# Two-block layer on one core: attention values taken transposed in column halves, softmax weights put on the exponentials

## Chip, cores and metric

The kernel runs on one core of one Trainium2 chip, as one launch. The metric is the device time in microseconds (us); where several runs are shown it is their median. A profile shows one execution of the program, with its own time and span.

## What is computed

The layer has two blocks. Only the second one's attention is touched. Its input is 512 tokens in four tiles of 128. In short, from the reference:

```python
# NSA: 8 heads of 64 in 2 groups; three softmaxes per head, each with a gate
o = g[..., 0:1] * o_cmp + g[..., 1:2] * o_slc + g[..., 2:3] * o_win
# o_cmp: 31 compressed keys; o_slc, o_win: causal over up to 512 keys
# MLA: 8 heads, query/key width 96, value width 64
p = masked_softmax(s, key_idx[None, :] <= tc[:, None])
o_mla = jnp.einsum('bhqk,bkhd->bqhd', p, v)
mixed = jnp.concatenate([o_nsa * silu(z_nsa), o_mla * silu(z_mla)], axis=-1)
x = x + gate[:, None, :] * (mixed @ w_out[l])
```

For 512 keys the selection takes all blocks, so the branches slc and win are both plain causal attention with their own keys and values.

## The kernel before

The second block is `block2`. Its projections come first; then `attention()` (L1524) runs woven with `fill()` (L1809), and last `out_tiles((2, 3))` makes the output of two token tiles. TensorE's order inside the woven part is the program's order (`tc.manual_schedule` with that engine, L1842); the other engines are ordered by the scheduler.

**Attention.** The work is a list of units, `ORDER_2` (L1150). A `Unit` (L1364) is two heads of one token tile `tt` in one branch; it sees n = (tt+1)*128 keys. There are 8 units per tile for the two NSA branches ("key") and 4 per tile for MLA ("mla"), so 48 units, and one `Blocks` unit (L1401) per tile for the 31 compressed keys of all 8 heads. A unit has three steps:

- `scores`: two matmuls and two mask matmuls into two "sc" banks, two maxima on VectorE (L1380), two exponentials on ScalarE with their sums (L1383);
- `turn`: 128x128 transposes of the exponentials on TensorE (L1391), evacuated by `K.copy`, which takes ScalarE (L63) and VectorE (L65) by turns;
- `values`: per head and 128 keys one matmul (L1398) with the transposed exponentials as the stationary operand and 64 columns of values as the moving one. The result has tokens on partitions.

When the units of a branch are through, `nsa_done` (L1455) takes reciprocals of the sums, multiplies them by the gates and weighs the 128x512 result on VectorE (L1359); GpSimd adds the branches (L1467). For MLA `finish` (L1498) does the like (L1499, L1501). `mix` (L1548) then transposes four 128x128 pieces on TensorE (L1552), multiplies them by z on VectorE (L1555) and splits the product in two parts for the output projection.

**Pipeline.** `attention()` issues in one step: `turn` of the unit before, `scores` of this unit, fill, `values` of the unit two before (LAG = 1).

**Fill.** `fill()` is the other TensorE work: `latents` (7 projections, the first two of which give the gates), `blocks` (compressed keys; with a Silu at L1673 and a rope before the transpose L1700), four columns of z and a Silu of all of it (L1807), `heads` (MLA queries, keys, values), four more columns of z and the second Silu, then `mix` of the NSA tiles and `out_tiles((0, 1))`, which needs both NSA and MLA of tiles 0 and 1. A column is 24 matmuls of 512 columns (L105 to L107), written as 8 pieces of 0.64 us.

`weave_us` (L178) sets how they alternate: each step of attention yields a number of us (`u.us`, twice the number of `FB` in `ORDER_2`) and the fill is advanced until its own written costs have eaten it. Where a step needs something of the fill (`needs`: "gates", "blocks", "heads", "z") it yields 1.0 until that is done. Where the fill needs attention's results it yields `None`, and the step then gets no fill:

```python
while tt == 1 and ("mla", 1) not in done:
    yield None
if tt == 1:
    yield from out_tiles((0, 1))
```

**First block, for comparison.** Its attention (L351 on) already puts the reciprocal sums on the exponentials (L396) and takes values with tile positions (0, 0) and (0, 64) (L407), with a stationary operand of 64 columns and 128 moving columns, at K = 128 rows.

Of the kernel before, what the change touches and what calls it, by code (L numbers as in the profile page):

```python
# [23 lines left out]
NT = S // 128  # L24
# [1122 lines left out]
FB = (2.2, 1.6, 1.1, 0.8, 0.7, 0.7)  # L1147
LAG = 1
# [113 lines left out]
def block2(K, x, h, wq, out):  # L1262
    nc, tc, A = K.nc, K.tc, K.A
    with ExitStack() as ctx:
# [10 lines left out]
        oN = P.tile([128, NT, 512], F32, name="oN")  # L1275
# [4 lines left out]
        vc = P.tile([128, 2, 4, 64], F32, name="vc")  # L1280
        nc.gpsimd.memset(vc, 0.0)
# [71 lines left out]
        def pair_cols(hh):  # L1353
            j, g = hh % 4, hh // 4
            return slice(j * 128 + g * 64, j * 128 + (g + 1) * 64)

        def weigh(dst, o, f):

            nc.vector.tensor_tensor(dst.rearrange("p (j g d) -> p g j d", g=2, d=64),  # L1359
                                    o.rearrange("p (j g d) -> p g j d", g=2, d=64),  # L1360
                                    f.rearrange("p (g j) -> p g j", g=2)[:, :, :, None].to_broadcast([128, 2, 4, 64]),
                                    op=OP.mult)

        class Unit:  # L1364

            post = needs = None

            def __init__(self, tt, q, k, sums, v, o):
                self.tt, self.q, self.k, self.sums, self.v, self.o = tt, q, k, sums, v, o

            def scores(self):
# [9 lines left out]
                self.p = [T.tile([128, 512], F32, name="sm_p", bufs=2) for _ in range(2)]  # L1381
                for i in range(2):
                    nc.scalar.activation(self.p[i][:, :n], sc[i][:, :n], AF.Exp, bias=m[i], accum_out=self.sums[i])  # L1383

            def turn(self):
                n = (self.tt + 1) * 128
                self.pt = []
                for p in self.p:
                    tp = K.bank("tp")
                    for j in range(0, n, 128):  # L1390
                        nc.tensor.transpose(tp[:, j:j + 128], p[:, j:j + 128], K.ident)  # L1391
                    self.pt.append(T.tile([128, 512], F32, name="sm_pt", bufs=2 * LAG + 2))
                    K.copy(self.pt[-1][:, :n], tp[:, :n])

            def values(self):
                for i in range(2):
                    for kb in range(self.tt + 1):
                        nc.tensor.matmul(self.o(i), self.pt[i][:, kb * 128:(kb + 1) * 128], self.v(i, kb), start=kb == 0,  # L1398
                                         stop=kb == self.tt)

        class Blocks:  # L1401
# [3 lines left out]
            def __init__(self, tt, csum, o):  # L1405
                self.tt, self.csum, self.o = tt, csum, o

            def scores(self):
# [11 lines left out]
                pc = self.pc = T.tile([128, 512], F32, name="sm_p", bufs=2)[:, :256].rearrange("p (j n) -> p j n", n=32)  # L1420
                nc.gpsimd.memset(pc[:, :, NCMP:], 0.0)
                for g in range(2):
                    hs = slice(4 * g, 4 * g + 4)
                    nc.vector.tensor_reduce(cx[:, hs], p3[g], axis=AX.X, op=OP.max)
                    nc.vector.tensor_tensor(pc[:, hs, :NCMP], p3[g], cx[:, hs, None].to_broadcast([128, 4, NCMP]),
                                            op=OP.subtract)
                nc.scalar.activation(pc[:, :, :NCMP], pc[:, :, :NCMP], AF.Exp)
                nc.vector.tensor_reduce(self.csum, pc[:, :, :NCMP], axis=AX.X, op=OP.add)

            def turn(self):  # L1430
                tp = K.bank("tp")
                for g in range(2):
                    nc.tensor.transpose(tp[:, g * 128:(g + 1) * 128],
                                        self.pc[:, 4 * g:4 * g + 4].rearrange("p j n -> p (j n)"), K.ident)
                self.pt = T.tile([128, 512], F32, name="sm_pt", bufs=2 * LAG + 2)
                K.copy(self.pt[:, :256], tp[:, :256])

            def values(self):
                o = self.o().rearrange("p (j g d) -> p g j d", g=2, d=64)
                for g in range(2):  # L1440
                    nc.tensor.matmul(o[:, g], self.pt[:, g * 128:(g + 1) * 128], vc[:, g], start=True, stop=True)

        def shared_bank():

            got = []

            def get():
                if not got:
                    got.append(K.bank("o"))
                return got[0]  # L1450
            return get

        sums = T.tile([128, NT, 3, 8], F32, name="sums")

        def nsa_done(tt, br, o):  # L1455
            gl = gates[:, tt].rearrange("p (h b) -> p b h", b=3)
            f = sums[:, tt, br]
            nc.vector.reciprocal(f, f)
            if br == 0 and tt == 0:
                nc.vector.tensor_scalar(f, f, has, None, op0=OP.mult)  # L1460
            nc.vector.tensor_tensor(f, f, gl[:, br], op=OP.mult)
            if br == 1:
                weigh(oN[:, tt], o(), f)
            else:
                tmp = T.tile([128, 512], F32, name="otmp", bufs=2)
                weigh(tmp, o(), f)
                nc.gpsimd.tensor_tensor(oN[:, tt], oN[:, tt], tmp, op=OP.add)  # L1467
            if br == 0:
                done.add(("nsa", tt))

        def key_units(tt):

            ts = slice(tt * 128, (tt + 1) * 128)
            for br in range(2):
                o = shared_bank()
                for j in range(4):
                    gs = [slice(g * 64, (g + 1) * 64) for g in range(2)]
                    u = Unit(tt, [qn[g, j, ts] for g in gs], [kn[g, br, :(tt + 1) * 128] for g in gs],
                             [sums[:, tt, 1 + br, hh:hh + 1] for hh in (j, j + 4)],
# [482 lines left out]
```

## Time and profile before

| | us |
|---|---|
| median of 3 runs | 2116.11 |
| lowest and highest of these | 2109.63, 2116.51 |
| the profiled execution's own time | 2122.33 |
| its span, first to last instruction | 2120.5 |

Over the span TensorE is busy 95%, VectorE 74%, ScalarE 42%, GpSimd 23%. The second block's attention starts at 1784 us from the span's start; its last values matmul starts at 2089 us; the end is at 2120.5 us. In rows, PE is TensorE (PEld its weight loads), DVE is VectorE, ACT is ScalarE, POOL is GpSimd, SP is SyncE. A float32 matmul shows as two records. Records overlap, since a matmul's end includes its way through the array; what one costs in a dense stretch is read from start to start. "PEclk" is the granted share of TensorE's clock: 1.00 is 2.4 GHz, and a stretch at 1.2 GHz counts half.

### The profile page before, as it was taken

How to read it: one execution, taken by the hardware profiler on the slowest of the kernel's cores; microseconds unless marked ns; L12 is line 12 of the kernel's file. 1: busy time of each engine (PE TensorE's matmuls, PEld its weight loads, DVE VectorE, ACT ScalarE, POOL GpSimd, SP SyncE). 2: the span in 40 equal slices, each digit the busy share in tenths (PEclk: the TensorE clock that was granted, in tenths of full speed). 3: DMA queues.
4: the chain of work that ended last, by engine and by line, in shares of the span. 5: the costliest groups of instructions: out<-in, count | busy, mean ns of one | idle time of the engine just before them, and what ended most of it. 6: DMA issues, size and time to landing. Idle time of an engine off the chain costs nothing.

```text
span 2120.5 us, 29959 instructions
## 1 busy us (share of the span) xinstructions
PE 2004.2 (95%) x11204; PEld 1717.0 (81%) x11204; DVE 1568.4 (74%) x3062; ACT 889.3 (42%) x1389; POOL 487.5 (23%) x408
## 2 busy tenths in 40 slices
PE   8989899999777888999999999999999999999998
PEld 6767676888777878999999999999988877777776
DVE  4557875479999996877777778787878775545557
ACT  4454433333324776333333333333334443444544
POOL 0000002210442000444444444444422001011000
PEclk9999999999888999999999999999999999999899
DMA  4214443432232557999899998999978762211012
GB/s 152 79 58 140 133 136 99 186 118 75 80 90 95 214 213 260 326 320 329 312 328 311 326 332 306 337 309 328 321 259 314 256 213 72 65 40 51 30 51 79
DMA packets 154377, 410.50 MB, mean 194 GB/s; under 512 B 13789, under 2 KB 63733, under 8 KB 150774
## 3 DMA queue, kind: packets, MB, share of 16 engines
q1 hardware_dynamic: 113332, 247.07, 34.5%
q0 software_dynamic: 37440, 136.33, 18.7%
q10 hardware_dynamic: 3458, 25.17, 3.1%
q8 instruction: 88, 1.44, 0.3%
q14 instruction: 59, 0.48, 0.1%
HBM read 378.64 MB, written 29.37 MB: 192 GB/s over the span
## 4 chain that ended last, share of the span: by engine, by line
PE 74%; DVE 16%; ACT 3%; DMA 3%; issue 3%; POOL 1%; DVEq 0%; ACTq 0%; POOLq 0%
PE ps_mm L105 12%; PE ps_mm L107 12%; PE ps_mm L106 12%; PE ps_o L105 6%; PE ps_o L107 6%; PE ps_o L106 6%; PE ps_tp L106 3%; PE ps_tp L107 3%; PE ps_tp L105 3%; PE ps_o L1398 2%; DMA raw<-in_ada_w_dram 2%; PE ps_sc L1375 2%; DVE wlo L69 2%; DVE ohG L982 2%; DVE hot L978 2%
## 5 line engine op out<-in xcount | busy, mean ns | idle before, releaser
L68 ACT ACTIVATE whi<-raw 128x1024 fp32r<-128x1024 f32 (+1 forms) x363 | 382.6, 1056 | 643.1 <-issue 450.8
L69 DVE TENSOR_TENSOR wlo<-raw,whi 128x1024 fp32r<-128x1024 f32 (+1 forms) x339 | 415.0, 1226 | 185.1 <-ACT whi L68 183.5
L105 PE MATMUL ps_o<-hT_hi,whi 128*128 128x384 f32 x992 | 343.1, 346 | 12.2 <-ACT act L729 12.2
L107 PE MATMUL ps_o<-hT_hi,wlo 128*128 128x384 f32 x992 | 337.3, 340 | 0.1
L106 PE MATMUL ps_o<-hT_lo,whi 128*128 128x384 f32 x992 | 336.6, 339 | 0.0
L1036 POOL DMA_INDIRECT gath<-in_peer_u_dram,idx x128 | 180.0, 1406 | 376.8 <-DVE junk L1044 174.8
L1036 POOL DMA_INDIRECT gath<-in_peer_v_dram,idx x128 | 176.1, 1376 | 257.8 <-DVE acc L1051 209.3
L105 PE MATMUL ps_mm<-hT_hi,whi 128*128 128x512 f32 (+1 forms) x544 | 221.9, 408 | 0.0
L107 PE MATMUL ps_mm<-hT_hi,wlo 128*128 128x512 f32 (+1 forms) x544 | 215.2, 396 | 0.0
L106 PE MATMUL ps_mm<-hT_lo,whi 128*128 128x512 f32 (+1 forms) x544 | 214.7, 395 | 0.0
L105 PEld LDWEIGHTS ps_o<-hT_hi,whi 128*128 128x128 f32 x992 | 190.2, 192 | 16.1 <-ACT act L729 12.8
L107 PE MATMUL ps_mm<-whi,wl 128*128 128x512 f32 x512 | 202.2, 395 | 0.0
L105 PE MATMUL ps_mm<-whi,wh 128*128 128x512 f32 x512 | 200.1, 391 | 2.1 <-ACT wh L68 2.1
L106 PE MATMUL ps_mm<-wlo,wh 128*128 128x512 f32 x512 | 201.6, 394 | 0.4 <-DVE wlo L69 0.4
L106 PEld LDWEIGHTS ps_o<-hT_lo,whi 128*128 128x128 f32 x992 | 190.0, 191 | 3.3
L107 PEld LDWEIGHTS ps_o<-hT_hi,wlo 128*128 128x128 f32 x992 | 189.4, 191 | 0.9 <-POOL wlo L69 0.5
L1051 DVE SCALAR_TENSOR_TENSOR acc<-gath,w,acc 128x1024 f32<-128x1024 f32 x127 | 162.7, 1281 | 6.8 <-DMA gath<-in_peer_v_dram,idx 4.6
L1044 DVE SCALAR_TENSOR_TENSOR junk<-gath,h 128x1024 bf16<-128x1024 f32 x128 | 156.5, 1223 | 8.9 <-DMA gath<-in_peer_u_dram,idx 6.4
L107 PEld LDWEIGHTS ps_mm<-hT_hi,wlo 128*128 128x128 f32 (+1 forms) x544 | 103.1, 189 | 23.3
L105 PEld LDWEIGHTS ps_mm<-hT_hi,whi 128*128 128x128 f32 (+1 forms) x544 | 103.5, 190 | 21.7 <-issue 0.6
L1006 ACT ACTIVATE gst<-ps_mm 128x512 f32<-128x512 f32 x96 | 104.0, 1123 | 40.2 <-PE ps_mm L1004 39.9
L106 PEld LDWEIGHTS ps_mm<-hT_lo,whi 128*128 128x128 f32 (+1 forms) x544 | 103.6, 190 | 20.6 <-DVE hT_lo L69 0.2
(482 smaller groups left out, 3546.7 us busy)
## 6 DMA issues: line engine op xcount, KB each, us to landing
raw<-in_peer_uT_dram SPq DMA_DIRECT2D x128, 512.0 KB
raw<-in_peer_v_dram SPq DMA_DIRECT2D x128, 512.0 KB
raw<-in_w_in_dram SPq DMA_DIRECT2D x59, 512.0 KB
gates_dram<-gst ACTq DMA_DIRECT2D x24, 1024.0 KB
x<-gates_dram SPq DMA_DIRECT2D x32, 768.0 KB
raw<-in_ada_w_dram SPq DMA_DIRECT2D x24, 512.0 KB
raw<-in_w_out_dram SPq DMA_DIRECT2D x24, 512.0 KB
raw<-in_w_peer_q_dram SPq DMA_DIRECT2D x16, 512.0 KB
```

Of the source, the lines that this page charges most:

```text
L68: self.nc.scalar.activation(hi, src, AF.Copy)
L69: (engine or self.nc.vector).tensor_tensor(lo, src, hi.bitcast(F32), op=OP.subtract)
L105: mm(out, a[0], b[0], start=start, stop=False)
L106: mm(out, a[0], b[1], start=False, stop=False)
L107: mm(out, a[1], b[0], start=False, stop=stop)
L978: nc.vector.tensor_tensor(hot.rearrange("p c j e i -> p (c j) e i"), iota_e[:, None].to_broadcast([128, 2 * pr, PK, 2]), ikT[:, ch].rearra ...
L982: nc.vector.tensor_tensor(Ag, hot[:, 0:1].to_broadcast([128, 3, pr, PK, 2]), g3T[:, ch].rearrange("p c (j i) -> p c j i", i=2)[:, :, :, No ...
L1006: nc.scalar.activation(st[:, :, t0:t0 + 4].rearrange("p a t -> p t a"), p.rearrange("p (t a) -> p t a", t=4), AF.Copy)
L1036: nc.gpsimd.indirect_dma_start(out=gath[i], out_offset=None, in_=A["peer_u" if i < NG // 2 else "peer_v"], in_offset=bass.IndirectOffsetOn ...
L1044: nc.vector.scalar_tensor_tensor(junk, g, 1.0, h0, op0=OP.mult, op1=OP.mult, accum_out=act0[:, k:k + 1])
L1051: nc.vector.scalar_tensor_tensor(acc0, g, w0[:, k:k + 1], acc0, op0=OP.mult, op1=OP.add)
L1375: nc.tensor.matmul(sc[i][:, :n], self.q[i], self.k[i], start=True, stop=False)
```

## The change

1. `values` swaps the operands: 64 columns of values are stationary, 128 tokens of transposed exponentials move. Head 0 writes partitions 0 to 63 and head 1 partitions 64 to 127 of one bank (tile positions (0, 0) and (0, 64)). The result is transposed already, so `mix` has no transposes, and all three NSA branches of a tile add up in one bank.
2. A new step `weigh` multiplies the exponentials by reciprocal sum and gate before `turn`. The weighing of results and GpSimd's additions go away; a copy from the bank to oN (NSA) is new.
3. `turn` and `values` come two steps behind `scores` (LAG = 2), `weigh` one step; `values` after a quarter of the step's fill. Every key unit now needs the gates before the next unit's scores.
4. `FB` has other numbers. The wait for "z" and the mix of MLA tiles 0 and 1 are done together behind tile 1.
5. `Blocks` transposes each head's 31 columns by itself (8 transposes, not 2), and its values are two matmuls of 512 columns; the compressed values are made once and not four times.

```diff
-FB = (2.2, 1.6, 1.1, 0.8, 0.7, 0.7)
-LAG = 1
+FB = (1.25, 1.25, 1.2, 1.0, 0.75, 0.7)
+LAG = 2
...
+        class Bank:
...
+            def add(self, i, cols, v, pt, stop):
+                start = self.p is None
+                if start:
+                    self.p, self.begun = K.bank("o"), set()
+                nc.tensor.matmul(self.p[i * 64:(i + 1) * 64, cols], v, pt, start=i not in self.begun, stop=stop,
+                                 tile_position=(0, i * 64))
+                self.begun.add(i)
...
+            def weigh(self):
+                n = (self.tt + 1) * 128
+                nc.vector.reciprocal(self.sum, self.sum)
+                if self.gate is not None:
+                    nc.vector.tensor_tensor(self.sum, self.sum, self.gate, op=OP.mult)
+                for i, p in enumerate(self.p):
+                    nc.vector.tensor_scalar(p[:, :n], p[:, :n], self.sum[:, i:i + 1], None, op0=OP.mult)
...
             def values(self):
-                for i in range(2):
-                    for kb in range(self.tt + 1):
-                        nc.tensor.matmul(self.o(i), self.pt[i][:, kb * 128:(kb + 1) * 128], self.v(i, kb), start=kb == 0,
-                                         stop=kb == self.tt)
+                cs = slice(self.pair * 128, (self.pair + 1) * 128)
+                for kb in range(self.tt + 1):
+                    for i in range(2):
+                        self.o.add(i, cs, self.v(i, kb), self.pt[i][:, kb * 128:(kb + 1) * 128], self.last and kb == self.tt)
...
             def turn(self):
-                tp = K.bank("tp")
+                self.pt = []
                 for g in range(2):
-                    nc.tensor.transpose(tp[:, g * 128:(g + 1) * 128],
-                                        self.pc[:, 4 * g:4 * g + 4].rearrange("p j n -> p (j n)"), K.ident)
-                self.pt = T.tile([128, 512], F32, name="sm_pt", bufs=2 * LAG + 2)
-                K.copy(self.pt[:, :256], tp[:, :256])
+                    tp = K.bank("tp")
+                    for j in range(4):
+                        nc.tensor.transpose(tp[:NCMP, j * 128:(j + 1) * 128], self.pc[:, 4 * g + j], K.ident)
+                    self.pt.append(T.tile([128, 512], F32, name="sm_pt", bufs=4))
+                    K.copy(self.pt[g][:NCMP], tp[:NCMP])
...
+        def nsa_done(tt):
+            K.copy(oN[:, tt], banks[tt].p.rearrange("p (j t) -> p j t", j=4))
+            done.add(("nsa", tt))
...
             def finish():
-                nc.vector.reciprocal(ms, ms)
-                oM = T.tile([128, 512], F32, name="otmp", bufs=2)
-                nc.vector.tensor_tensor(oM.rearrange("p (h d) -> p h d", d=64), o().rearrange("p (h d) -> p h d", d=64),
-                                        ms[:, :, None].to_broadcast([128, 8, 64]), op=OP.mult)
-                return lambda: (mix(tt, oM, 4), done.add(("mla", tt)))
+                while "z" not in done:
+                    yield 1.0
+                while late["mixes"] and late["mixes"][0][0] <= tt:
+                    t, b = late["mixes"].pop(0)
+                    mix(t, b.p.rearrange("p (j t) -> p j t", j=4), 4)
+                    done.add(("mla", t))
...
+                while u and u.needs == "blocks" and u.needs not in done:
                     yield 1.0
-                if line[0]:
-                    line[0].turn()
+                while line[0] and line[0].needs and line[0].needs not in done:
+                    yield 1.0
+                if line[-1]:
+                    line[-1].turn()
                 if u:
                     u.scores()
...
+                if line[0]:
+                    line[0].weigh()
+                us = u.us if u else 2.0
+                yield us * 0.25
+                if line[-1]:
+                    line[-1].values()
+                    yield from line[-1].post and line[-1].post() or ()
+                yield us * 0.75
+                line = [u] + line[:-1]
...
-            p = K.bank("tp")
-            for j in range(4):
-                nc.tensor.transpose(p[:, j * 128:(j + 1) * 128], o[:, j * 128:(j + 1) * 128], K.ident)
...
-            nc.vector.tensor_tensor(mt, p.rearrange("p (j t) -> p j t", j=4), late["z"][k0 // 4][:, :, ts], op=OP.mult)
+            nc.vector.tensor_tensor(mt, o, late["z"][k0 // 4][:, :, ts], op=OP.mult)
```

## Rows read from the trace of the kernel before

**Rows 1.** Windows: per engine busy us (x instructions), then PEclk, DMA share, GB/s.
```profile
1840.00:1856.00 16.00, 12.47 (x124) 9.50 (x123) 7.35 (x19) 8.29 (x21) 1.91 (x3) 0.89 0.17 53
1880.00:1900.00 20.00, 16.49 (x97) 15.17 (x96) 9.15 (x33) 11.87 (x19) 2.86 (x10) 0.74 0.10 27
1980.00:2004.00 24.00, 19.52 (x93) 13.21 (x91) 11.78 (x20) 13.40 (x26) 0.00 (x0) 0.72 0.07 23
2004.00:2090.00 86.00, 85.58 (x565) 68.58 (x564) 51.84 (x90) 43.09 (x96) 2.65 (x3) 1.00 0.15 50
```

**Rows 2.** Waits of TensorE, 1784 to 2121 us: total us, times, longest us.
```profile
PE ps_mm L105 <- ACT qm L1721: 3.5, 1, 3.5
...
PE ps_tp L1391 <- ACT sm_pt L63: 2.5, 1, 2.5
PE ps_mm L1676 <- issue: 2.0, 1, 2.0
PE ps_tp L1700 <- DVE kct L1227: 1.5, 1, 1.5
```

**Rows 3.** Timeline of TensorE: values of a unit of tile 2, now (start, busy us).
```profile
1939.60 1.45 PE L1398 MATMUL ps_o<-vn,sm_pt 128*128 128x64 f32 x12
1940.88 0.82 PE L1391 MATMUL ps_tp<-ident,sm_p 128*128 128x128 f32 x6
```

**Rows 4.** Timeline of TensorE, first block: values on column halves, and their neighbours.
```profile
67.33 0.44 PE L407 MATMUL ps_o<-sm_pt,av 128*64 128x128 f32 x4
67.69 0.49 PE L371 MATMUL ps_sc<-kT,qT 64*128 64x128 f32 x4
...
184.61 0.50 PE L105 MATMUL ps_mm<-hT_hi,whi 128*128 128x512 f32 x1
185.04 0.66 PE L407 MATMUL ps_o<-sm_pt,av 128*64 128x128 f32 x8
185.63 0.50 PE L106 MATMUL ps_mm<-hT_lo,whi 128*128 128x512 f32 x1
185.97 0.39 PE L107 MATMUL ps_mm<-hT_hi,wlo 128*128 128x512 f32 x1
186.20 0.40 PE L105 MATMUL ps_mm<-hT_hi,whi 128*128 128x512 f32 x1
```

**Rows 5.** Timeline of TensorE: the transposes of one mix.
```profile
2075.40 0.60 PE L1552 MATMUL ps_tp<-ident,otmp 128*128 128x128 f32 x4
2075.83 0.33 PE L1398 MATMUL ps_o<-vm,sm_pt 128*128 128x64 f32 x2
```

**Rows 6.** VectorE by form, 1784 to 2121 us: weighing of results (count, busy, mean ns).
```profile
L1359 DVE TENSOR_TENSOR otmp<-ps_o,sums 128x512 f32<-128x512 f32 x8 | 5.5, 687 | 2.9 <-issue 2.1 <-PE ps_o L1441 0.3 <-PE ps_o L1398 0.3
...
L1359 DVE TENSOR_TENSOR oN<-ps_o,sums 128x512 f32<-128x512 f32 x4 | 2.8, 692 | 6.3 <-PE ps_o L1398 6.2
L1501 DVE TENSOR_TENSOR otmp<-ps_o,ms 128x512 f32<-128x512 f32 x4 | 2.8, 688 | 3.9 <-issue 3.4 <-PE ps_o L1398 0.5
```

**Rows 7.** VectorE by form, first block, 0 to 420 us: what resembles the new step.
```profile
L396 DVE TENSOR_SCALAR sm_p<-sm_p,es 128x256 f32<-128x256 f32 x24 | 7.5, 350 | 0.4
...
L393 DVE RECIPROCAL es<-es 128x2 f32<-128x2 f32 x16 | 2.6, 166 | 0.5
...
L326 DVE TENSOR_SCALAR lf<-lf,omlb,lb 128x512 f32<-128x512 f32 x4 | 2.0, 540 | 0.2 <-ACT lf L324 0.2
L396 DVE TENSOR_SCALAR sm_p<-sm_p,es 128x128 f32<-128x128 f32 x8 | 1.9, 283 | 0.1
```

**Rows 8.** Timeline of VectorE in a step of tile 3 (idle before in brackets).
```profile
2019.67 0.69 DVE L65 COPY sm_pt<-ps_tp 128x512 f32<-128x512 f32 x1 [2.83 <-PE ps_tp L1391]
```

**Rows 9.** Timeline of ScalarE at the second Silu of z.
```profile
1981.51 1.28 ACT L1807 ACT_TABLE_LOAD   x1
1982.80 1.91 ACT L1807 ACTIVATE z<-z 128x2048 f32<-128x2048 f32 x1
1984.62 1.14 ACT L68 ACTIVATE hT_hi<-mt 128x512 fp32r<-128x512 f32 x2
```

More of the change, by code (lines that the diff above doesn't have):

```diff
@@ new lines, in weigh @@
+            def weigh(self):
+                f = T.tile([128, 8], F32, name="cf", bufs=2)
+                nc.vector.tensor_reduce(f, self.pc, axis=AX.X, op=OP.add)
+                nc.vector.reciprocal(f, f)
+                if self.tt == 0:
+                    nc.vector.tensor_scalar(f, f, has, None, op0=OP.mult)
+                nc.vector.tensor_tensor(f, f, branch(self.tt, 0), op=OP.mult)
+                nc.vector.tensor_tensor(self.pc, self.pc, f[:, :, None].to_broadcast([128, 8, NCMP]), op=OP.mult)
@@ L1438, in values @@
             def values(self):
-                o = self.o().rearrange("p (j g d) -> p g j d", g=2, d=64)
                 for g in range(2):
[L1441 to L1469, printed above, removed]
+                    self.o.add(g, slice(0, 512), vc[:NCMP, g * 64:(g + 1) * 64], self.pt[g][:NCMP], True)
@@ L1471, in key_units, with branch @@
+        def branch(tt, br):
+            return gates[:, tt].rearrange("p (h b) -> p b h", b=3)[:, br]
+        banks = [Bank() for _ in range(NT)]
+        def nsa_done(tt):
+            K.copy(oN[:, tt], banks[tt].p.rearrange("p (j t) -> p j t", j=4))
+            done.add(("nsa", tt))
         def key_units(tt):
@@ L1524, in attention @@
         def attention():
-            line, after = [None] * (LAG + 1), None
-            for u in itertools.chain(units(), (None,) * (LAG + 2)):
+            line = [None] * LAG
+            for u in itertools.chain(units(), (None,) * LAG):
                 if isinstance(u, float):
@@ L1691, in blocks @@
                 for g in range(2):
-                    for j in range(4):
-                        nc.tensor.matmul(p[j * 32:j * 32 + NCMP, g * 64:(g + 1) * 64], cols(1, g), w2[:, 1], start=True,
-                                         stop=True)
-                for j in range(4):
-                    js = slice(j * 32, j * 32 + NCMP)
-                    K.copy(vc[js, :, j], p[js, :128].rearrange("p (g d) -> p g d", g=2))
+                    nc.tensor.matmul(p[:NCMP, g * 64:(g + 1) * 64], cols(1, g), w2[:, 1], start=True, stop=True)
+                nc.vector.tensor_copy(vc[:NCMP], p[:NCMP, :128])
                 yield 0.64
```

74 lines of the change are left out of this document (24 added, 50 removed).

## Prediction

> **What bounds it now.** I first read the windows over the second block's attention. From 2004 to 2090 us TensorE is busy 85.58 of 86 us at full clock [rows 1]: there TensorE's own instructions set the pace, and an instruction saved is time saved. VectorE is busy 51.84 of those 86 us, 60%. Three windows look otherwise [rows 1]. At 1840 to 1856 TensorE is idle 16 - 12.47 = 3.5 us, at 1880 to 1900 3.5 us, at 1980 to 2004 4.5 us, and the granted clock is 0.89, 0.74 and 0.72: part of each ran at 1.2 GHz after the idle time, which cost 0.11*16 = 1.8, 0.26*20 = 5.2 and 0.28*24 = 6.7 us of work. Together that is at most 25.2 us, the second thing the change can touch. The waits tell why [rows 2]: the first projection of the MLA heads waits 3.5 us for ScalarE, busy with the first Silu; a transpose waits 2.5 us because ScalarE does the second Silu before it empties the bank; the Silu and rope of the compressed keys cost 2.0 and 1.5.
>
> The third window is also a matter of order. Adding the written costs of the fill, z is complete at 98 us of fill; the steps before the first MLA unit ask for 8*4.4 + 8*3.2 + 2*3.2 + 8*2.2 + 2.2 = 87, and the eight MLA units of tiles 0 and 1 for 12.8. So the fill reaches its `None` (MLA of tile 1 not done) when that tile's last units are not yet issued, and five steps run without any fill, with scores, maximum, exponential and transpose behind each other.
>
> **Part 1, values swapped.** A call issues 4, 8, 12 or 16 records for tile 0 to 3, and there are 12 calls of each: 480 records. Now 12 records take 1940.88 - 1939.60 = 1.28 us, 0.107 each [rows 3]; in all 51.2 us. No row of this attention shows the new form, but the first block has it exactly, 64 stationary columns, 128 moving ones, halves alternating [rows 4]: 4 records take 67.69 - 67.33 = 0.36 us, 8 take 185.63 - 185.04 = 0.59. So a pair of records costs 0.115 and each call 0.13 more; 12 and 16 records make 0.82 and 1.05. Twelve of each: 12*(0.36 + 0.59 + 0.82 + 1.05) = 33.8 us. The neighbours pay as well: the projection matmul between two such calls takes 185.04 - 184.61 = 0.43, the one behind them 185.97 - 185.63 = 0.34, an undisturbed one 186.20 - 185.97 = 0.23 [rows 4]. So about 0.1 is lost going in and 0.1 coming out. Following the written costs, in 33 of the 48 calls fill stands on both sides (0.2), in 15 the call comes directly behind its step's scores, after which the fill's first matmul is slow anyway (0.1): 33*0.2 + 15*0.1 = 8.1 us. The saving is 51.2 - 33.8 - 8.1 = **9.3 us**. Bounds: 17.4 if the edges cost nothing more than now, 6 if all calls pay 0.2 and the first one of each 0.05 more. I take the middle count because it rests on the same form on the same engine.
>
> The Trainium skill's page "TensorEngine Tiling (Array Packing)", sections "Theoretical Speedup" and "Stationary-Streaming Swap + Column Tiling", allows up to 2x for such a swap; the sum would then have 25.6 us here and not 9.3. Its section "Key Properties" speaks against that: changing the tiling mode drains TensorE. By that rule the edges above are real, and the trace agrees (0.43 and 0.34 against 0.23).
>
> **Part 2, other TensorE work.** The mix transposes go: eight mixes of 2075.83 - 2075.40 = 0.43 [rows 5], 3.4 us. `Blocks` issues 32 transposes and not 8; at the same 0.11 each that is 24 more, 2.6 us. Bounds zero (they are only 31 columns wide) and 2.6; I take 2.6 since 128 columns still move. Its values keep their column count and the compressed values lose six short matmuls: nothing, well under 0.5 either way. Parts 1 and 2: 9.3 + 3.4 - 2.6 = **10.1 us** less on TensorE.
>
> **Part 3, weighing on the exponentials.** Per unit: a reciprocal of two columns, a gate product (key units), two scalings. First-block prices [rows 7]: reciprocal 0.166, scaling of 256 columns 7.5/24 = 0.31, of 128 1.9/8 = 0.24; 512 columns of a similar form 2.0/4 = 0.50; 384 about 0.41. With 24 scalings of each width 35 us, 48 reciprocals 8, 32 gate products at the reciprocal's price 5.3: 48 us on VectorE. Gone are 5.5 + 2.8 + 2.8 = 11.1 us of weighing results [rows 6] and GpSimd's additions. Net some 37 us over about 300. The cover is VectorE's idle time: in a tile-3 step it waits 2.83 us before its copy [rows 8], and the step adds 2*0.50 + 2*0.166 = 1.33. So I cost it at nothing in throughput. It is the order that may cost: VectorE works in order, and now the copy of the transposes must be ready after only this step's scores (about 1.1 to 1.3 us for 512 keys), not one whole step later. Behind a scaling or a split of weights the copy is late and TensorE waits. Bounds: 0, and 1.33 in each of 24 steps (tile 2 and 3 key units, tile 2 and 3 MLA), 32 us. I take 3, near the low end because of rows 8.
>
> **Part 4, order of the fill.** The steps before the first MLA unit now ask for 66.6 us. The key units' new wait for the gates runs some 9 us of dense projections ahead at the start, at no loss. Then "heads" holds the attention for four yields while transposes wait for evacuations: I take a loss of 1.3, between 0 and 2.5 (the longest wait of a transpose now [rows 2]). z completes just after tile 1's last values, so the fill's `None` phase disappears. But the new place has its own wait: the first output matmul needs the product of oN and z split, h's buffer is reused for it and free only after the last z matmul, and in ScalarE's order the Silu stands before: table 1.28, Silu 1.91, split half of 1.14 [rows 9], and before and behind them VectorE's copy and low part, 0.7 each like the other 512-column instructions [rows 6], 5.2 us together, with nothing between on TensorE. With some 3 us for the clock behind it, 8.2 replaces 4.5 + 6.7 = 11.2: 3 us gained. At the first Silu, one unit's transposes and scores (about 1.5 us) now stand between the z column and the projections, so of the 3.5 idle and 5.2 of clock I take off 3.5. At the compressed keys the Silu's 2.0 gets cover, the copy behind loses it: 1.5 gained. At the end five drain steps have no fill; the last output tiles can cover most, 1.5 lost. No weight load is late: the stream is fetched three granules ahead and the order of its SP issues is kept; GpSimd's queue only gets shorter.
>
> **Sum.** -10.1 (TensorE) + 3 (copies) + 1.3 - 3 - 3.5 - 1.5 + 1.5 = -12.3 us. The profiled execution's own time is 2122.3, so 2110.0; it stands 6.2 us above the median of the runs, 2116.1. The predicted median is **2104 us**.
>
> **Rivals.**
>
> - *The three pauses close almost wholly.* If the split goes ahead of the Silu on ScalarE, and the first Silu finds enough attention work, most of the 25.2 us [rows 1] goes: -10.1 - 25.2 + 5 = -30, 2086 us. For it: no None phase. Against: both Silus still stand in ScalarE's one queue. Chance 0.13.
> - *Column halves give the full factor two*, by the page's rule: -12.3 - 16.3, about 2087.5 us. The first block's rows speak against it. Chance 0.04.
> - *Nothing to be seen.* The edges take the upper price (6 us saved, not 9.3), and the second Silu's wait with its clock keeps all 11.2: -12.3 + 3.3 + 3 = -6, 2110 us; with copies a little later, up to 2116. Chance 0.22.
> - *Slower: VectorE's queue sets the step.* If in the 24 steps of tiles 2 and 3 the scaling stands before the copy, each waits up to 1.33: -12.3 - 3 + 32 = +17, 2133; at two thirds of that, 2122. It decides when the copy starts later than the end of the step's scores. For it: the split of a weight granule and the maxima share that queue. Against: 60% busy [rows 1], 2.83 idle [rows 8]. Chance 0.11.
>
> **Numbers.** The forecast has 0.50. About 0.3% (6.3 us) is what a measurement of this kernel tells from no change, so faster means below 2109.8: forecast and the two fast rivals, 0.67; same 0.22; slower 0.11. The range, 2087 to 2115, takes in the bounds of part 1, the pauses closing nearly or not at all, and leaves out the slower rival.
>
> **What would show it.** Right: value records in near-simultaneous pairs, a call of 16 in about 1.05 us, 0.43 and 0.34 beside them; no L1552 rows; no fill-less stretch; one pause of about 5 us behind the second Silu; full clock in tile 3's steps. Wrong: TensorE waiting for the copy (L65) or the scaling in most steps of tile 3; a call of 16 above 1.4 us; a granted clock below 0.9 in new windows.

## The result, and the profile after

The changed kernel ran at a median of **2107.11 us** (2105.22 to 2111.26, 14 runs) beside 2115.94 us (2109.63 to 2124.40, 14 runs) for the kernel before on the same chip. The ratio on record is 0.9949, with a 95% interval of 0.9938 to 0.9960 (the quotient of the two medians alone is 0.9958): some 9 to 11 us less. The forecast was 2104, its range 2087 to 2115. The profiled execution took 2105.86 us, with a span of 2103.6; the one of before took 2122.33.

More than a third of the difference of the two profiled executions lies ahead of the change: the second block's first scores start at 1784.0 us before and at 1778.1 after, in code that the change doesn't touch. The granted clock there accounts for most of these 5.9 us: counting time at 1.2 GHz half, that stretch lost 34.1 us before and 29.0 after. Other profiles below start the second block between 1778 and 1786. So I compare from the first scores to the end of VectorE's last instruction, 3.3 us before the span's end in both, in windows (columns as in [rows 1]). Before:

```profile
1784.00:2117.20 333.20, 312.20 (x1921) 249.33 (x1920) 186.28 (x418) 155.15 (x357) 23.35 (x45) 0.95 0.18 57
```

After, first the whole, then the three places of the pauses and the steps of tile 3 that answer to [rows 1]:

```profile
1778.10:2100.30 322.20, 299.36 (x1901) 211.94 (x1900) 214.73 (x565) 156.69 (x359) 12.74 (x33) 0.97 0.18 59
...
1846.00:1862.00 16.00, 13.25 (x100) 9.06 (x99) 7.72 (x29) 6.83 (x19) 0.62 (x2) 0.79 0.11 33
1894.00:1903.00 9.00, 5.88 (x30) 4.47 (x24) 3.60 (x14) 6.18 (x10) 1.44 (x4) 0.81 0.13 51
1980.00:1998.00 18.00, 13.68 (x75) 8.61 (x73) 13.13 (x27) 12.87 (x20) 0.00 (x0) 0.91 0.10 30
2004.00:2072.00 68.00, 67.65 (x476) 47.49 (x475) 52.13 (x111) 35.47 (x82) 0.00 (x0) 1.00 0.15 49
```

This stretch went from 333.2 to 322.2 us: **-11.0 us**. VectorE's work grew from 186.3 to 214.7 us, and yet tile 3 runs as before: TensorE busy 67.65 of 68 us at full clock, VectorE 77% busy there instead of 60%. The first Silu (second of the four rows) lost 3.1 us idle and 0.19*9 = 1.7 by the clock, 4.8 instead of 8.7 us; the second Silu 4.3 + 0.09*18 = 5.9 instead of 11.2; the compressed keys 2.8 + 0.21*16 = 6.1 instead of 5.3.

To see which part is TensorE's own work, I add up the time from each matmul's start to the next one's, without the gaps in which it stood idle, and count time at the lower of the two clock levels (1.2 GHz) half. What remains is idle time, and the time lost by the clock; some 5 us follow the last matmul in each kernel. This "own work" differs by 0.1 us between two profiles of the changed kernel (290.8 and 290.9).

| from the first scores on, us | before | after | moved | forecast |
|---|---|---|---|---|
| values of the pairs (L1398, now L1362) | 51.5 | 34.9 | -16.6 | -17.4 |
| their neighbours: L105 to L107 and the masks (L1377, now L1379) | 145.4 | 155.8 | +10.4 | +8.1 |
| mix transposes (L1552) | 3.7 | 0 | -3.7 | -3.4 |
| transposes of `Blocks` (L1433, now L1453) | 1.0 | 3.7 | +2.7 | +2.6 |
| TensorE's own work in all | 297.3 | 290.8 | **-6.5** | -10.1 |
| TensorE idle | 15.9 | 17.7 | +1.8 | |
| lost by the clock | 14.5 | 8.2 | **-6.3** | |

In any other group of matmuls half a microsecond or less moved, but for the transposes of the pairs (-0.7; a pair is the two heads of a unit). A call of values, that is, the values of one pair, in TensorE's timeline (start, busy, then what it is):

```profile
2003.89 0.29 PE L1379 MATMUL ps_sc<-cmask,identb 128*128 128x128 bf16 x2
2004.10 1.09 PE L1362 MATMUL ps_o<-sm_pt,vn 128*64 128x128 f32 x16
2005.13 0.50 PE L105 MATMUL ps_mm<-whi,hT_hi 128*128 128x512 f32 x1
2005.46 0.39 PE L106 MATMUL ps_mm<-wlo,hT_hi 128*128 128x512 f32 x1
2005.69 0.39 PE L107 MATMUL ps_mm<-whi,hT_lo 128*128 128x512 f32 x1
```

From start to start 16 records take 1.03 us (forecast 1.05), where 12 took 1.28 before [rows 3]. The matmul behind them takes 0.33 and the next ones 0.23. Calls of 4, 8 and 12 records took 0.37, 0.59 and 0.81: 0.15 for the call, and 0.109 for each two records.

The waits of TensorE from 1778 us on (total us, times, longest), beside [rows 2]:

```profile
PE ps_mm L105 <- ACT hT_hi L68: 4.1, 2, 2.7
PE ps_mm L105 <- ACT qm L1709: 3.1, 1, 3.1
PE ps_tp L1402 <- ACT sm_pt L63: 1.9, 2, 1.2
PE ps_tp L1688 <- DVE kct L1227: 1.8, 1, 1.8
...
PE ps_tp L1402 <- DVE sm_pt L65: 1.1, 1, 1.1
...
PE ps_o L1362 <- ACT sm_pt L63: 0.5, 1, 0.5
...
PE ps_tp L1402 <- DVE sm_p L1394: 0.2, 1, 0.2
```

and one more of the kernel before:

```profile
PE ps_tp L1391 <- ACT sm_p L1383: 2.8, 3, 1.4
```

The new scaling (L1394) held TensorE once, for 0.2 us. The copies (L63, L65) held the next transposes, which need the bank, three times, in all 3.0 us (before, L63 alone held them 2.5 [rows 2]); they held the values, which read what was copied, once, for 0.5. The waits of the transposes for exponentials, 2.8 us before, are gone: with the second step a pair's exponentials are a step older when it is turned. At the second Silu ScalarE's timeline reads

```profile
1985.14 0.62 ACT L68 ACTIVATE hT_hi<-mt 128x512 fp32r<-128x512 f32 x1
1985.77 1.28 ACT L1795 ACT_TABLE_LOAD   x1
1987.07 1.92 ACT L1795 ACTIVATE z<-z 128x2048 f32<-128x2048 f32 x1
...
1991.22 1.28 ACT L1386 ACT_TABLE_LOAD   x1
...
1993.19 0.62 ACT L68 ACTIVATE hT_hi<-mt 128x512 fp32r<-128x512 f32 x1
```

and TensorE's

```profile
1985.81 0.50 PE L105 MATMUL ps_mm<-whi,hT_hi 128*128 128x512 f32 x1 [1.43 <-ACT hT_hi L68]
...
1993.86 0.50 PE L105 MATMUL ps_mm<-whi,hT_hi 128*128 128x512 f32 x1 [2.69 <-ACT hT_hi L68]
```

The split for the first output product stands ahead of the table load, not behind the Silu as I had taken it. So the product waits 1.43 us; the split of the second query tile comes after the Silu, two more mixes and the exponential's table load, and costs 2.69.

### The profile page after: what moved, and what is told of

Read it like the earlier page. It is cut to its first block, busy times and chain, and to the rows that moved or that the text cites. A ratio compares the mean times of both kernels' runs of the same rounds, so it can differ in the third digit from the quotient of the medians.

```text
span 2103.6 us, 29961 instructions
## 1 busy us (share of the span) xinstructions
PE 1985.4 (94%) x11184; PEld 1675.0 (80%) x11184; DVE 1596.6 (76%) x3209; ACT 891.1 (42%) x1391; POOL 479.2 (23%) x395
## 3 DMA queue, kind: packets, MB, share of 16 engines
q8 instruction: 87, 1.43, 0.3%
## 4 chain that ended last, share of the span: by engine, by line
PE 75%; DVE 15%; ACT 4%; DMA 3%; issue 2%; POOL 1%; ACTq 0%; DVEq 0%; POOLq 0%
PE ps_mm L105 12%; PE ps_mm L106 12%; PE ps_mm L107 12%; PE ps_o L105 7%; PE ps_o L107 7%; PE ps_o L106 7%; PE ps_tp L107 3%; PE ps_tp L105 3%; PE ps_tp L106 3%; PE ps_mm L1004 3%; DMA raw<-in_ada_w_dram 2%; DVE wlo L69 2%; PE ps_sc L1377 1%; PE ps_o L1362 1%; DVE sum L895 1%
## 5 line engine op out<-in xcount | busy, mean ns | idle before, releaser
L105 PE MATMUL ps_o<-hT_hi,whi 128*128 128x384 f32 x992 | 342.4, 345 | 12.7 <-ACT act L729 12.7
L107 PE MATMUL ps_o<-hT_hi,wlo 128*128 128x384 f32 x992 | 336.8, 340 | 0.1
L105 PE MATMUL ps_mm<-hT_hi,whi 128*128 128x512 f32 (+1 forms) x544 | 224.2, 413 | 0.0
L107 PE MATMUL ps_mm<-hT_hi,wlo 128*128 128x512 f32 (+1 forms) x544 | 214.7, 395 | 0.0
L105 PEld LDWEIGHTS ps_o<-hT_hi,whi 128*128 128x128 f32 x992 | 189.6, 191 | 16.6 <-ACT act L729 13.3
L105 PE MATMUL ps_mm<-whi,wh 128*128 128x512 f32 x512 | 200.2, 391 | 2.0 <-ACT wh L68 2.0
L107 PE MATMUL ps_mm<-whi,wl 128*128 128x512 f32 x512 | 201.8, 394 | 0.0
L107 PEld LDWEIGHTS ps_o<-hT_hi,wlo 128*128 128x128 f32 x992 | 188.8, 190 | 1.2 <-POOL wlo L69 0.8
L105 PEld LDWEIGHTS ps_mm<-hT_hi,whi 128*128 128x128 f32 (+1 forms) x544 | 102.9, 189 | 26.8 <-issue 6.9
L107 PEld LDWEIGHTS ps_mm<-hT_hi,wlo 128*128 128x128 f32 (+1 forms) x544 | 102.5, 188 | 23.2
```

The lines of the kernel that those rows point to most:

```text
L105: mm(out, a[0], b[0], start=start, stop=False)
L107: mm(out, a[1], b[0], start=False, stop=stop)
```

## The experiments

The theory to test: the gain is TensorE's shorter work (values, mixes) less the edges of the calls, plus shorter pauses; VectorE's new work lies beside it. The rivals: the schedule alone (fill or second step) makes the gain; VectorE's queue takes much of it. Eleven kernels ran. Each row's last four columns are from its profile, from the first scores on, as in the table above.

| kernel | median us (range, runs) | ratio to before (95%) | length | own work | idle | clock |
|---|---|---|---|---|---|---|
| changed, run again | 2107.28 (2104.74 to 2113.06, 6) | 0.9951 (0.9933, 0.9968) | 320.1 | 290.9 | 17.5 | 6.2 |
| old fill | 2106.56 (2103.37 to 2109.38, 8) | 0.9954 (0.9939, 0.9968) | 321.1 | 289.7 | 16.1 | 9.7 |
| one step | 2136.43 (2134.41 to 2140.79, 4) | 1.0098 (1.0071, 1.0126) | 351.7 | 291.9 | 36.8 | 16.4 |
| no scaling | 2100.51 (2098.26 to 2108.20, 6) | 0.9931 (0.9909, 0.9954) | 316.6 | 290.3 | 14.0 | 6.7 |
| halves in turn | 2109.62 (2108.37 to 2113.15, 10) | 0.9975 (0.9963, 0.9988) | 323.3 | 299.7 | 16.3 | 1.7 |
| before, even fill | 2114.10 (2110.19 to 2120.17, 10) | 0.9984 (0.9968, 1.0001) | 327.3 | 297.7 | 14.4 | 9.7 |
| keys of 0, 1 first | 2107.60 (2105.94 to 2109.84, 7) | 0.9954 (0.9937, 0.9971) | 319.1 | 291.8 | 15.6 | 6.2 |
| paired values | 2101.67 (2099.91 to 2107.19, 5) | 0.9934 (0.9910, 0.9957) | 313.9 | 282.7 | 17.8 | 7.9 |
| both of these | 2104.24 (2101.96 to 2108.16, 7) | 0.9943 (0.9924, 0.9963) | 317.9 | 282.7 | 18.2 | 11.5 |
| quad values | 2099.95 (2096.73 to 2103.70, 6) | 0.9920 (0.9900, 0.9939) | 312.6 | 280.9 | 18.0 | 8.2 |
| paired, ScalarE scales | 2107.43 (2105.39 to 2108.07, 6) | 0.9953 (0.9936, 0.9971) | 320.8 | 281.7 | 22.8 | 10.9 |

**The fill, undone and done alone.**

```diff
-FB = (1.25, 1.25, 1.2, 1.0, 0.75, 0.7)
+FB = (2.2, 1.6, 1.1, 0.8, 0.7, 0.7)
```

> The changed kernel with the old planner times FB = (2.2, 1.6, 1.1, .8, .7, .7), all else kept. Theory (the gain comes from what TensorE no longer does in the values and the mixes, and the even fill is worth only the pauses that it shortens: the first Silu lost 4.8 us of pause and half clock with the even fill and 8.7 without it): 2 to 4 us above the changed kernel, some 2110 us, the first Silu's loss back near 8.7 us. Rival 1 (the spread makes the gain): back at the time before, 2114 to 2118 us. Rival 2 (the spread is worth nothing): within 1 us of 2107 us.

The old fill in the changed kernel made no difference: 2106.56 beside 2107.11 us. Its ratio, 0.9954, stands inside the interval of the changed kernel's. And the loss moved to another place than I expected. The first Silu kept its short pause; the second Silu got its long one back:

```profile
1870.00:1885.00 15.00, 11.95 (x76) 9.44 (x73) 8.90 (x32) 11.70 (x22) 2.96 (x9) 0.89 0.13 35
1960.00:1985.00 25.00, 19.77 (x97) 13.43 (x96) 13.50 (x41) 14.54 (x38) 0.00 (x0) 0.73 0.07 22
```

That is 3.1 + 0.11*15 = 4.7 us, and 5.2 + 0.27*25 = 12.0 (after: 5.9). So the even fill does shorten the second Silu's pause, and loses the same elsewhere: idle and clock together are 25.8 us with the old fill and 25.9 with the new one (23.7 in its second profile).

> The kernel before with the new planner times FB = (1.25, 1.25, 1.2, 1.0, .75, .7) alone. Theory (the spread is worth only the shorter pauses at the first Silu and the compressed keys, some 3 to 4 us): 2111 to 2114 us. Rival 1 (the spread makes the whole gain): 2105 to 2109 us. Rival 2 (worth nothing without the second pipeline step): 2115 to 2118 us.

The kernel before with the even fill alone: 2114.10 beside 2118.34 us for before on that chip, a ratio whose interval just reaches 1. It fits 3 to 4 us; it is not settled against nothing. The whole gain it is not: TensorE's own work stays at 297.7 us.

This kernel is also the nearest neighbour of the changed one, since both have the same fill numbers. From it to the changed kernel's two profiles own work falls by 6.8 to 6.9 us, idle and clock together go from 24.1 to 25.9 and 23.7, and the median falls from 2114.10 to 2107.11 and 2107.28, by 7 us (as much by the ratios, though the chips differ). With the fill held the same, then, the gain is TensorE's shorter work.

**One pipeline step.**

```diff
-LAG = 2
+LAG = 1
...
+                if LAG == 1 and line[0]:
+                    line[0].weigh()
                 if line[-1]:
                     line[-1].turn()
...
-                if line[0]:
+                if LAG > 1 and line[0]:
                     line[0].weigh()
```

> The changed kernel with one pipeline step in place of two (LAG = 1): a pair is turned in the step behind its scores, and its weighing on VectorE stands between. Theory (at two steps VectorE's weighing held TensorE for 0.2 us in all; at one step the maxima, exponentials and weighing of a pair, some 3.5 to 4 us at 512 keys, have to end within the 3.2 us that a step of 4.8 us leaves between its scores and the next transposes): little in the first tiles, 0.5 to 1 us of waiting in each of some 20 steps at 384 and 512 keys, 2115 to 2123 us, with waits of L1402 and its like on sm_p of 8 to 16 us. Rival (the second step is not needed): within 1.5 us of 2107 us.

29 us slower than the changed kernel, and 20 slower than before, above the range that I expected. The wait was the expected one, at a higher price. (LAG also sets the number of buffers for exponentials, 2*LAG: this kernel has two, like the one before, and not four. No run separates the buffers from the step.) TensorE's waits:

```profile
PE ps_tp L1402 <- DVE sm_p L1394: 21.4, 18, 3.9
...
PE ps_tp L1402 <- DVE kr L1225: 2.8, 1, 2.8
```

and VectorE's timeline in one step of tile 3:

```profile
2021.82 1.28 DVE L1382 TENSOR_REDUCE nm<-ps_sc 128x1 f32<-128x512 f32 x2
2024.02 0.17 DVE L1390 RECIPROCAL sm_s<-sm_s 128x2 f32<-128x2 f32 x1 [0.92 <-ACT sm_p L1386]
2024.22 0.16 DVE L1392 TENSOR_TENSOR sm_s<-sm_s,gates 128x2 f32<-128x2 f32 x1
2024.41 0.88 DVE L1394 TENSOR_SCALAR sm_p<-sm_p,sm_s 128x512 f32<-128x512 f32 x2
```

From the start of the maxima to the end of the scaling 25.29 - 21.82 = 3.5 us pass, and TensorE's next transposes waited 1.12 us for it. The idle time grew by 19 us, the loss by the clock by 8. Weighing on the exponentials pays here only with the second step, which hides it: the two parts of the change belong together.

**No scaling** (reciprocal and gate stay).

```diff
-                for i, p in enumerate(self.p):
-                    nc.vector.tensor_scalar(p[:, :n], p[:, :n], self.sum[:, i:i + 1], None, op0=OP.mult)
```

> The changed kernel without the two scalings of the exponentials by sum and gate in a pair's weighing (the reciprocal and the gate stay, the products of the pairs are left out, so the attention is not normalised). It takes some 30 us of VectorE's work out. Theory (TensorE sets the time; the scaling held it 0.2 us in the changed kernel): 0 to 3 us below the changed kernel, 2104 to 2107 us. Rival (VectorE's queue sets the time from tile 3 on): 10 us or more below, under 2097 us.

2100.51 us, 6.6 below the changed kernel's median. The two ran on different chips: by the ratios to before it is 3.8 us, with intervals that overlap, and by the profiles 3.5 to 5.6. All of these lie above my bound of 3 and below the rival's 10. VectorE's work fell by 214.7 - 184.8 = 29.9 us and TensorE's idle time by 3.7. The waits at the second Silu moved:

```profile
PE ps_mm L105 <- ACT hT_hi L68: 1.8, 2, 1.4
...
PE ps_mm L107 <- DVE hT_lo L69: 1.0, 2, 0.6
```

The waits for splits fell from 4.1 to 1.8, and 1.0 for their low parts is new; the waits at the first Silu, the compressed keys and the copies stand within 0.1 of what they were. ScalarE's timeline shows why:

```profile
1991.51 0.63 ACT L68 ACTIVATE hT_hi<-mt 128x512 fp32r<-128x512 f32 x1 [1.77 <-DVE mt L1545]
1992.16 1.28 ACT L1386 ACT_TABLE_LOAD   x1
```

The split of the second query tile now stands ahead of the exponential's table load; in the changed kernel it stood behind it. It isn't a queue of scalings that held it there: between 1985.6 and 1994.9 us no scaling ran in the changed kernel. So a kernel without the scalings is 3.5 to 6.6 us shorter, but with their removal the order on ScalarE changed too, and no run separates the two.

**Column halves in turn**, not alternating.

```diff
-                for kb in range(self.tt + 1):
-                    for i in range(2):
+                for i in range(2):
+                    for kb in range(self.tt + 1):
```

> The changed kernel with the loops of the values exchanged: all key tiles of the one column half first, then all of the other, same records. Theory (two records take 109 ns together because they stand on different column halves and alternate): a call of 16 records goes from 1.02 to about 1.9 us, and 416 records of 128 columns cost 55 ns more each, 23 us in all, 2125 to 2131 us. Rival (a half-width record costs half, in whatever order): calls of 1.02 us and 2107 us.

Both expectations fell. TensorE's timeline, a call of 8 and one of 16, each with the start of the next matmul:

```profile
1864.32 0.66 PE L1362 MATMUL ps_o<-sm_pt,vn 128*64 128x128 f32 x8
1864.92 0.50 PE L105 MATMUL ps_mm<-hT_hi,whi 128*128 128x512 f32 x1
...
2001.84 1.58 PE L1362 MATMUL ps_o<-sm_pt,vn 128*64 128x128 f32 x16
2003.35 0.50 PE L105 MATMUL ps_mm<-whi,hT_hi 128*128 128x512 f32 x1
```

8 records take 0.60 us, as when alternating; 16 take 1.51, between 1.03 and the 1.86 of one after the other (0.15 + 16*0.107); 12 took 1.08. TensorE's own work grew by 8.9 us (twelve calls of 12 by 0.27, twelve of 16 by 0.49: 9.1). The medians are only 2.3 to 2.5 us apart (5 by the ratios), and in this profile the clock cost 1.7 us and not 6 to 8. That denser work kept the clock up is argued and not shown: over whole executions the time lost by the clock (span times one minus the granted clock) is 38.4 us on average here, and 41.2 and 40.4 in the changed kernel's two sets of runs.

**The edges of the calls.**

```diff
-            line = [None] * LAG
+            line, held = [None] * LAG, []
...
-                    line[-1].values()
+                    held.append(line[-1])
+                    if len(held) == 2 or line[-1].post:
+                        for w in held:
+                            w.values()
+                        held = []
```

> The changed kernel with the values of two pairs in one call: a pair's values are held until the next pair has been turned, so 28 calls stand where 52 stood, with the same records. Theory (each call costs an edge of its own: the matmul ahead of it takes 0.10 us more, its first two records 0.15 us more than the later ones, and the matmul behind it 0.10 us more): 24 calls less at some 0.33 us, 5 to 8 us below the changed kernel, 2099 to 2102 us. Rival 1 (the 0.15 us belongs to the first record of each accumulation, not to the call): 24 at 0.2 us, some 2102 to 2103 us. Rival 2 (the later values keep the transposes' buffers, and the copies wait for them): 2107 us or more.

2101.67 us. TensorE's own work fell from 290.8 to 282.7: 8.1 us for 24 calls, 0.34 a call, what the theory gave. A joined call and its neighbours:

```profile
2006.46 0.40 PE L107 MATMUL ps_mm<-whi,hT_lo 128*128 128x512 f32 x1
2006.78 1.97 PE L1362 MATMUL ps_o<-sm_pt,vn 128*64 128x128 f32 x32
2008.68 0.50 PE L105 MATMUL ps_mm<-whi,hT_hi 128*128 128x512 f32 x1
2009.02 0.39 PE L106 MATMUL ps_mm<-wlo,hT_hi 128*128 128x512 f32 x1
```

32 records take 1.90 = 0.15 + 16*0.109, with 0.32 and 0.34 at its two sides: one edge where two were. Values of four pairs in tiles 0 and 1 go one further (there one buffer takes both heads of a pair):

```diff
-                    if len(held) == 2 or line[-1].post:
+                    if len(held) == (4 if line[-1].tt < 2 else 2) or line[-1].post:
...
+                if self.tt < 2:
+                    tp = K.bank("tp")
+                    for i, p in enumerate(self.p):
+                        for j in range(0, n, 128):
+                            nc.tensor.transpose(tp[:, i * n + j:i * n + j + 128], p[:, j:j + 128], K.ident)
+                    pt = T.tile([128, 512], F32, name="sm_pt", bufs=4)
+                    K.copy(pt[:, :2 * n], tp[:, :2 * n])
+                    self.pt = [pt[:, :n], pt[:, n:2 * n]]
+                    return
```

> Values of two pairs in one call, and in the first two query tiles of four pairs: there both heads of a pair are turned into one bank and copied as one, so that four buffers hold four pairs. 22 calls in place of the changed kernel's 52, same records. Theory (an edge of some 0.33 us per call; the paired kernel gave back 8.1 us of TensorE's own time at full clock for 24 calls): 30 calls less, 10 us of TensorE's time less than in the changed kernel, some 6 to 9 us of it on the end, 2098 to 2101 us. Rival (fewer, longer calls leave the fill in lumps, and the pauses grow): no lower than the paired kernel's 2102 us.

2099.95 us, and 2107.28 for the changed kernel run again on the same chip; the ranges (2096.73 to 2103.70, 2104.74 to 2113.06) don't meet. TensorE's own work is 280.9, another 1.8 less for six calls. This version beats both kernels: 0.992 of the time before.

> The changed kernel as it is, beside the three that follow on the same chip, as their measure. All theories: 2105 to 2109 us.

**The second Silu.**

```diff
-                while ("nsa", tt) not in done:
+                while tt != 1 and ("nsa", max(tt, 1)) not in done:
                     yield None
-                mix(tt, oN[:, tt], 0)
+                if tt != 1:
+                    mix(tt, oN[:, tt], 0)
+                if tt == 0:
+                    mix(1, oN[:, 1], 0)
```

> The changed kernel with the mixes of the second half's first two query tiles (oN of tiles 0 and 1, which need only the first z) both emitted ahead of the two mixes that need the second Silu. Theory (in the changed kernel the second output product waited 2.7 us for a split whose mix stood behind the two that waited for the Silu): that wait goes, 1.5 to 3 us below the changed kernel, some 2105 us. Rival (the pause only moves to the next product, which waits for the mixes behind): within 1 us of 2107 us.

The wait went as expected, from 4.1 us in two waits to one of 1.4:

```profile
PE ps_mm L105 <- ACT hT_hi L68: 1.4, 1, 1.4
```

The run did not become shorter: 2107.60. Between first scores and end the profile has 319.1 us, beside 322.2 and 320.1 for the two profiles of the changed kernel; a gain of 1 to 3 us there would drown in where that stretch begins (1785.3 here). Whether it is there stays open.

> The two edits together: the values of two pairs in one call, and the mixes of the first two query tiles ahead of the second Silu. Theory: the two gains add, 2 + 6 us below the changed kernel, 2097 to 2101 us. Rival (what one saves is idle time that the other had saved as well): no lower than the better of the two.

The gains did not add: 2104.24, no better than the paired kernel. TensorE's own work is the same 282.7; the clock cost 11.5 us, not 7.9.

**One scaling to ScalarE**, on top of the paired values.

```diff
-                for i, p in enumerate(self.p):
-                    nc.vector.tensor_scalar(p[:, :n], p[:, :n], self.sum[:, i:i + 1], None, op0=OP.mult)
+                p, r = self.p
+                nc.vector.tensor_scalar(p[:, :n], p[:, :n], self.sum[:, 0:1], None, op0=OP.mult)
+                nc.scalar.activation(r[:, :n], r[:, :n], AF.Copy, scale=self.sum[:, 1:2])
```

> Values of two pairs in one call, and of the two scalings of a pair one moved from VectorE to ScalarE (an activation by the column of sums): some 15 us of VectorE's work go to ScalarE, 44% busy there. Theory (without any scaling the changed kernel ran 6 us faster, its waits at the second Silu 4.1 to 1.8 us: VectorE's queue delays the splits there): 1 to 3 us below the paired kernel, 2099 to 2101 us. Rival (the scaling stands behind the next pair's exponentials on ScalarE, which hold TensorE instead): 2104 us or more, with waits of the transposes on ScalarE's sm_p.

5.8 us slower than the paired kernel by the medians (4 by the ratios, on another chip): the rival's time, for the most part by another wait than it named.

```profile
PE ps_mm L105 <- ACT hT_hi L68: 5.5, 2, 4.8
PE ps_mm L105 <- ACT qm L1714: 4.1, 1, 4.1
PE ps_mm L1673 <- ACT hid L1670: 3.4, 1, 3.4
...
PE ps_tp L1403 <- ACT sm_p L1395: 1.2, 1, 1.2
```

The scaled exponentials held TensorE 1.2 us. More came from the places where ScalarE is the last link anyway: 5.5 for the splits (3.4 in the paired kernel), 3.4 for the Silu of the compressed keys.

## Why the prediction was right, and where its terms were off

The sign and the size held: a sum of -12.3 us forecast, -11.0 between first scores and end, and -8.8 between the medians. It held because errors cancelled, which is luck: TensorE's own work gave 6.5 us and not 10.1, while idle time and clock together fell by 4.5 and not by the 2.2 that the other terms of the sum add up to. The median forecast rests besides on one profile of the kernel before, 6.2 us above its median; the profile of the changed kernel lies 1.25 below its own.

- **Part 1, values swapped: right in mechanism, the edges too small.** The calls came out within 0.02 us of the forecast (1.03 for 1.05, 0.81 for 0.82). The term that was mis-sized is the edges: 8.1 us forecast; the neighbours grew by 10.4. So the swap saved 16.6 - 10.4 = 6.2 us and not 9.3, near its lower bound (given as 6; with 0.25 for each of 48 calls, 17.4 - 12 = 5.4). In the 15 calls behind their own scores I charged only one side. The mask matmul in front pays as well: its group went from 4.8 to 6.5. The paired kernel is the direct measure: a call costs 0.34 us beyond its records, 0.15 of it inside the call.
- **The rival of the full factor two.** Beyond the call's 0.15 us, two records take 0.109 where one took 0.107 [rows 3]: for the records alone it is a factor of 1.96. A call of 16 gets 16*0.107/1.03 = 1.66, and the edges take 10.4 of the 16.6 us. The Trainium skill, page "TensorEngine Tiling (Array Packing)", section "Theoretical Speedup", gives "up to 2x": the trace agrees for the records. Its section "Key Properties" says that changing the tiling mode drains TensorE: the edges fit that (0.32 and 0.34 us in the rows of the joined call, beside 0.23), though no run shows that a drain is their cause.
- **Part 2: right.** The mix transposes gave 3.7 (forecast 3.4), those of `Blocks` cost 2.7 (2.6).
- **Parts 1 and 2 together** gave 6.5 us, not 10.1: the edges (2.3), the values themselves (0.8), and small moves in other groups.
- **Part 3, weighing: the price right, the place wrong.** The step that failed is "the copy of the transposes must be ready after only this step's scores". A copy held the values once, for 0.5 us; the copies held the next transposes 3.0 us, about as before, and the scaling 0.2. The second step took away 2.8 us of waits for exponentials; 1.3 of them lay in the window of the second Silu, the rest the sum had nowhere. The work itself was near the forecast: 29.9 us vanish with the scalings (forecast 35). "Nothing in throughput" is in doubt: without them the run is 3.5 to 6.6 us shorter, but that kernel has another order at the second Silu, with 2.3 us less waiting for splits; VectorE's busy share of 77% in tile 3 says nothing of it. The slower rival fell: tile 3 ran without pauses at two steps. At one step such waits came, 21.4 us of them.
- **Part 4.** First Silu: -3.9 us measured, -3.5 forecast; but with the old fill it is as short (4.7), so it is not the even fill that shortens it. Second Silu: -5.3 instead of -3, by two pauses and not one of 5.2 us, since ScalarE took the first split ahead of the Silu; the time at half clock behind them was 3.4 us, 1.6 us lost where 3 were forecast. Compressed keys: +0.8 instead of -1.5; the wait for their rope (1.8 us, before 1.5 [rows 2]) got no cover. The three places together gave -8.4 us (forecast -8.0); idle time and clock as a whole moved by -4.5, so 3.9 us were lost elsewhere, where copies, the heads' wait and the end had 5.8 in the sum. Which of these three it was I did not take apart.
- **Even fill** was one of the change's named parts, and it alone shows no gain in the changed kernel; in the kernel before it shows 4 us, not settled against nothing. The step that I had wrong is to add up the pauses one by one: moved fill shortens one and lengthens others.

What stays open: how the remaining 26 us of idle time and clock loss divide among orders of the same work, and how much of the 6.3 us by the clock belongs to the change. The granted clock of every execution is known, for the whole program, most of whose loss lies ahead of the change (29 to 44 us in the profiles). The time lost by it, reckoned as above, is 46.0 to 47.9 us on average in the kernel before (50 executions on three chips), and 41.2 and 40.4 in the changed one (14 and 6), but 47.1 and 46.5 in the faster paired and quad kernels (5 and 6). So a better clock came with this kernel and not with all that contain the change. No run separates a pause from the clock's answer to it, none gave the kernel before the second step alone, and none undid the swap alone.

## What to carry to other kernels

Count an operand swap onto column halves by calls, not only by columns: here each call cost 0.34 us beside records at half price, so the next gain lay in joining calls (8.1 us of TensorE's work for 24 calls), which no extra buffer was needed for. When a step goes on an engine "with idle time", ask which chains end on TensorE through that engine, and remove the step once to see its price, looking whether the order of the other engines changed with it; and when weighing moves ahead of a transpose, move the pipeline with it, or pay for the chain at every step.

## What the runs showed of the hardware

**What an edge is.** TensorE's weight loads at the call of values shown above (2004.10) and behind it:

```profile
2004.10 0.85 PEld L1362 LDWEIGHTS ps_o<-sm_pt,vn 128*64 128x64 f32 x16
2005.13 0.19 PEld L105 LDWEIGHTS ps_mm<-whi,hT_hi 128*128 128x128 f32 x1 [0.17 <-issue]
2005.23 0.19 PEld L106 LDWEIGHTS ps_mm<-wlo,hT_hi 128*128 128x128 f32 x1
```

and at a call of the kernel before:

```profile
1939.37 1.54 PEld L1398 LDWEIGHTS ps_o<-vn,sm_pt 128*128 128x128 f32 x12
```

In a dense stretch a load starts about one matmul ahead of its own: 2005.23 for the matmul at 2005.46, and before the change 1939.37 for the first value matmul at 1939.60 [rows 3]. At both edges of a call on column halves it starts only with its matmul: 2004.10 with 2004.10, 2005.13 with 2005.13. It is so at every call of the changed kernel and of the paired one. The edges are where this overlap is lost.

**How far the halves run apart.** The two column halves need not alternate record by record. Eight records, four of each half one behind the other, took 0.60 us as when alternating; 12 (6 and 6) took 1.08 and 16 (8 and 8) took 1.51. In units of 0.109 us behind the call's 0.15 these are 4.1, 8.5 and 12.5, and if the second half's first record could start no sooner than beside the first half's last one, they would be 7, 11 and 15. The times fit if a record may start up to four records ahead of its place when its half is free: 4, 8 and 12 units.

The records taken one by one show the same. In the call of 16 at 2001.84 their starts form two series of eight, each with 0.16 us behind its first record and 0.109 behind every other one. The second series starts 0.493 us into the call, right behind the fifth record of the first (0.487). In every call of 12 it starts right behind the third record (0.275 and 0.269 us), in most calls of 8 behind the first (0.01). In the program's order the second half's first record is the fifth, seventh or ninth, so it starts beside the record four places ahead of it, and before later records of the first half. A record doesn't name its half; that the two series are the two halves is read from their even spacing. The Trainium skill, page "TensorEngine Tiling (Array Packing)", section "Key Properties", says that tiles work independently; these times agree, and bound how far.
